# A second expert layer: 256 latent tokens dense in split products, or 160 dense in whole products and 96 gathered

## The chip, the core and the metric

One core of a Trainium2 chip runs the whole program. The metric is the device time of one execution in microseconds (us); the profile's times are counted from the first instruction of the span.

## The reference, cut to what matters

Two layers of a shared trunk run over 256 context tokens and 256 latent tokens of width 1024. Each layer ends in a retrieval of single-neuron experts out of 16384. Every token has 8 heads, each picks 16 experts, and what is added to the token is

```
u = jnp.take(expert_u, experts, axis=0)
v = jnp.take(expert_v, experts, axis=0)
act = jax.nn.gelu(jnp.einsum('td,ted->te', xb, u))
return jnp.einsum('te,ted->td', act * g, v)
```

where `g` is a softmax over the 16 scores of a head. In the second layer only the latent tokens go through this, and a last norm over them gives the output.

## The kernel before, in words

There are two ways to compute the experts, and both give the same sums. The dense way multiplies every expert with every token. A table A (tokens by experts, mostly zeros) holds the weights `g`, so that the output is (gelu(u x) * A) v. The gather way fetches the rows of a token's own experts: an indirect DMA on POOL's queue brings, for one of the 128 picks, one row of 4 KB for each of 128 tokens; VectorE multiplies and sums the row with the token (u), or adds it, scaled, to the token's sum (v).

In the first layer the context tokens go the gather way (`gather`, L1144) and the latents the dense way; the gather runs beside the latents' work. In the second layer all 256 latents go the dense way.

The dense way runs over 32 blocks of 512 experts. `hidden` (L978) makes one block of gelu(u x): four tiles of 512 KB of expert_ut, each with two of the eight slices of the contraction. The weights are TensorE's standing operand (128 experts), the 256 tokens stream. `value` (L1019) uses one block: four tiles of 512 KB of expert_v; here A's 128 tokens stand and 512 columns of v stream, for two token blocks and two halves of the width, into four accumulators in PSUM (`acc[b, h]`) that live through all 32 blocks. `scale` (L1011) multiplies a block of gelu with its part of A.

In the first layer the operands are whole fp32 (`whole=True`, `len(hT) == 1`). In the second, every operand is split into a high and a low fp32r part (`cut`, L210: ScalarE copies the high part at L215, VectorE subtracts at L148), and `mm3` (L320) issues three products for each, at L328, L329 and L330; `value` does so for A too (L1032, L1033) and issues its products at L1051.

`build` (L936) makes A from the picks, in chunks of 2, 3 and 3 parts of 16; for eight tokens at a time VectorE makes marks (L951 to L956), TensorE sums them with 16 small products (L964) and ScalarE writes them out (L966).

`peer_out` (L1054) writes the order. It first finishes the hidden blocks up to block 11, woven with the first chunk of A; then comes a loop over i = 0 to 31: `scale(i)`, `hidden(i + 8)` as long as there is one (from block 12 on, so in 20 of the 32 turns), and `value(i)`. After every tile's DMA a `step()` draws on the tasks beside: the builds of the other two chunks, and in the first layer the gather, each at a fixed rate for each step. Before `peer_out`, the heads' queries and picks (`peer_heads`) are woven with the first hidden blocks (`hiddens`), six in the second layer.

All dense tiles are loaded on SP's queue, in order. `dtile` (L193) takes four places of the pool "w" in turn; with whole operands every third tile comes from the pool "dw" instead. Each engine works through its own instructions in order. The gather has six places ("gx") and works four issues behind its newest (`lead`).

Of the kernel before, what the change touches and what calls it, by code (L numbers as in the profile page):

```python
# [36 lines left out]
NEG = -3.0e38  # L37

# [31 lines left out]
class Net:  # L70
# [690 lines left out]
    def peer_in(self, l, s, whole=False):  # L761
# [6 lines left out]
        st["hT"], st["done"] = hT, 0  # L768
        return st
# [166 lines left out]
    def build(self, st, s0, ns):  # L936

        j0, n = s0 * SUB, ns * SUB
        for i in range(ns):
            st["A", s0 + i] = self.va.tile([128, SUB, L], F32, name="A", bufs=4)  # L940
# [18 lines left out]
        def sums(ts, oi, oa):  # L959
            ps = self.psum()  # L960
            pv = ps[:, :TG * n].rearrange("p (t j) -> p t j", j=n)
            for u in range(TG):
                for i in range(2):
                    nc.tensor.matmul(pv[:, u, :], oi[:, u // TU, :, u % TU], oa[:, i, u // TU, :, u % TU], start=(i == 0), stop=(i == 1))  # L964
            for i in range(ns):
                nc.scalar.activation(st["A", s0 + i][:, :, ts].rearrange("p j t -> p t j"), pv[:, :, i * SUB:(i + 1) * SUB], AF.Copy, scale=1.0 / GS)  # L966
# [11 lines left out]
    def hidden(self, l, st, q):  # L978

        nc, hT = self.nc, st["hT"]  # L980
        ps = [self.psum() for i in range(2)]
        for k2 in range(4):
            w = self.dtile([128, 2, 512], len(hT) == 1)
            nc.sync.dma_start(w, self.t["expert_ut"][l, q, :, 2 * k2:2 * k2 + 2, :])
            u = (w,) if len(hT) == 1 else self.cut(w, [128, 2, 512])
            yield
            for kk in range(2):
                k = 2 * k2 + kk
                for j in range(4):

                    self.mm3(ps[j // 2][:, (j % 2) * L:(j % 2 + 1) * L], [x[:, kk, j * 128:(j + 1) * 128] for x in u], at_(hT, k),
                             k == 0 and j % 2 == 0, k == KD - 1)
        for i in range(2):
            if q < st.get("early", 0):
                if ("early", q // 4) not in st:
                    st["early", q // 4] = self.va.tile([128, SUB, L], F32, name="A", bufs=4)
                o = 4 * (q % 4) + 2 * i
                a = st["early", q // 4][:, o:o + 2, :]
            else:
                a = self.va.tile([128, 2, L], F32, name="act", bufs=2 * self.n["ahead"])  # L1000
            nc.scalar.activation(a, ps[i].rearrange("p (j t) -> p j t", j=2), AF.Gelu_apprx_tanh)  # L1001
            st["act", 2 * q + i] = a
# [16 lines left out]
    def value(self, l, acc, st, q, step):  # L1019

        nc, p = self.nc, self.vp
        A, o = st["A", 4 * q // SUB], 4 * q % SUB
        vt = self.t["expert_v"][l].rearrange("(j i) d -> i j d", i=NK)
        for j2 in range(2):
# [11 lines left out]
            for jj in range(2):  # L1036
# [9 lines left out]
                for x, b in todo:  # L1046
                    j = 4 * q + 2 * j2 + x
                    ts = slice(b * 128, (b + 1) * 128)
                    for n, (aa, ww) in enumerate(prods):
                        for h in range(2):  # L1050
                            nc.tensor.matmul(acc[b, h], aa[:, x, ts], v[x][ww][:, h * 512:(h + 1) * 512],  # L1051
                                             start=(j == 0 and n == 0), stop=(j == NK - 1 and n == len(prods) - 1))

    def peer_out(self, l, sets, late=None, beside=None, out=None):  # L1054
# [51 lines left out]
        for i in range(end):  # L1106
# [18 lines left out]
            elif i == end - 4 and l == DEPTH - 1:  # L1125

                self.gf, ga = [[self.va.tile([128, 512], F32, name="act", bufs=2 * ahead) for h in range(2)] for x in range(2)]
# [4 lines left out]
            if q == nq - 1:  # L1132
                for b in range(2):
                    for h in range(2):
                        nc.vector.tensor_tensor(out=acc[b, h], in0=acc[b, h], in1=ga[h], op=OP.mult)
                        xx = self.x[s, b][:, h * 512:(h + 1) * 512]
                        nc.vector.tensor_tensor(out=xx, in0=xx, in1=acc[b, h], op=OP.add)
                        self.square(s, b, h, xx, acc[b, h])
# [5 lines left out]
    def gather(self, l, s, st):  # L1144
# [9 lines left out]
        for row, col in zip(rows, (g, sh)):  # L1154
            self.row_of([row[:, 0:512], row[:, 512:D]], col)
        def room(name):
            return [self.pe.tile([128, D], F32, name=name, tag="hp", bufs=self.n["hp"]) for b in range(2)]
        hN, sums = room("hn"), None
        for b in range(2):
# [6 lines left out]
        jobs = [(w, b, r) for w in "uv" for r in range(nr) for b in range(2)]  # L1166
        tabs = {w: self.t["expert_" + w].rearrange("l e d -> (l e) d") for w in "uv"}
        got = []
        for i in range(len(jobs) + lead):
            if i < len(jobs):  # L1170
                w, b, r = jobs[i]
                x = gp.tile([128, D], F32, name="gx", bufs=n)
                nc.gpsimd.indirect_dma_start(x, None, tabs[w], bass.IndirectOffsetOnAxis(ap=idx[:, b, r:r + 1], axis=0),  # L1173
                                             element_offset=l * NK * NK * D)
                got.append(x)
            if i >= lead:
                w, b, r = jobs[i - lead]
                x = got.pop(0)
                if w == "u":
                    keep(nc.vector.tensor_tensor_reduce(out=x, in0=x, in1=hN[b], scale=1.0, scalar=0.0, op0=OP.mult, op1=OP.add,  # L1180
                                                        accum_out=coef[:, b, r:r + 1]))
                    if (r, b) == (nr - 1, 1):
                        nc.scalar.activation(coef, coef, AF.Gelu_apprx_tanh)
                        nc.vector.tensor_tensor(out=coef, in0=coef, in1=st["g"].rearrange("p b h r -> p b (h r)"), op=OP.mult)
                elif r == 0:
                    sums = sums or room("vsum")
                    nc.vector.tensor_scalar(sums[b], x, coef[:, b, 0:1], None, op0=OP.mult)
                else:
                    keep(nc.vector.scalar_tensor_tensor(sums[b], x, coef[:, b, r:r + 1], sums[b], op0=OP.mult, op1=OP.add))  # L1189
# [3 lines left out]
        for b in range(2):  # L1193
            nc.vector.tensor_tensor(out=sums[b], in0=sums[b], in1=ga, op=OP.mult)
            nc.vector.tensor_tensor(out=self.x[s, b], in0=self.x[s, b], in1=sums[b], op=OP.add)
# [5 lines left out]
        self.root(s, 2)  # L1201
# [15 lines left out]
def program(tc, t, out, dbg=None):  # L1217
    with ExitStack() as ctx:
# [18 lines left out]
        with pool("kc0") as net.kc:  # L1237
# [5 lines left out]
            net.n = dict(s1=2, b4=15, t4=4, s2=3, qz=1, hp=8, gt="hp", late=1, whole=1, gx=6, lead=4)  # L1243
# [9 lines left out]
        net.n = dict(s1=1, b4=4, t4=0, s2=2, hp=8, ahead=4, pre=4, gx=6, lead=4, dw=2)  # L1253
# [11 lines left out]
        with pool("pe1", "right") as net.pe:  # L1265
# [6 lines left out]
            net.n = dict(s1=1, b4=5, t4=0, s2=2, hp=4, ahead=8, pre=8)  # L1272
            wp = pool("wp2")
            net.wp = wp.__enter__()
            with pool("h1") as net.mp:
                sl = net.peer_in(1, "l")
                for _ in sl["fill"]:
                    pass
                run(net.by_head(net.peer_heads(1, "l", sl)), (net.hiddens(1, sl, 6), 3))
            net.io = None  # L1280
            with pool("v1") as net.vp:
                net.peer_out(1, [("l", sl)], out=out)
            wp.__exit__(None, None, None)
# [70 lines left out]
```

## Time and profile before

| | |
|---|---|
| three runs, median (range) | 3004.85 us (2996.38 to 3007.26) |
| the profiled execution | 2997.31 us, span 2995.5 us |
| busy TensorE, VectorE, ScalarE, POOL | 93%, 73%, 33%, 20% of the span |
| second layer, queries and picks | 2118 to 2307 us |
| second layer, rest of the hidden blocks | 2307 to 2377 us |
| second layer, loop over the value blocks | 2377 to 2986 us |
| first layer's loop, gather beside it | 957 to 1808 us |

PE is TensorE, PEld its load of the standing operand, DVE VectorE, ACT ScalarE. A whole fp32 product appears as two records (so 16 products as 32); `hph` and `hpl` are the high and low part of the tokens, `whi` and `wlo` those of the weights. [...] MB are millions of bytes.

### The profile page before, as it was taken

The numbers are of one execution on the slowest core, as the hardware profiler recorded it, in microseconds if no ns is written. First come the engines' busy times: TensorE is split into PE (matmuls) and PEld (weight loads), VectorE is DVE, ScalarE is ACT, GpSimd is POOL, SyncE is SP. The second block draws the span as 40 slices with busy tenths as digits, with TensorE's granted clock in tenths as the row PEclk, the third lists the DMA queues.
The fourth block names the chain that finished last, engine by engine and source line by source line (L and its number), as shares of the span: only waits on it lengthen the run. The fifth ranks groups of instructions, "written<-read, shape, count | busy, mean of one in ns | idle before, by whom it ended". The sixth has DMA issues, their size and how long they took to land.

```text
span 2995.5 us, 45775 instructions
## 1 busy us (share of the span) xinstructions
PE 2781.6 (93%) x17380; PEld 2232.5 (75%) x17380; DVE 2181.6 (73%) x4525; ACT 976.9 (33%) x1798; POOL 598.7 (20%) x528
## 2 busy tenths in 40 slices
PE   7999999977995899998999988899987999999998
PEld 3779787756883466665766637889887989999987
DVE  3656676767999787667976675866799978548755
ACT  4454312301113021001200005555533555446544
POOL 0000000056312555445755450000000000000000
PEclk8999999988996999999999999999998999999999
DMA  7664665599862999999999994444443555665564
GB/s 266 193 202 146 205 193 162 174 367 380 313 230 93 385 337 385 409 409 361 368 407 409 409 380 137 129 121 144 149 144 114 154 170 170 190 189 163 176 197 147
DMA packets 295708, 724.64 MB, mean 242 GB/s; under 512 B 26817, under 2 KB 147905, under 8 KB 295489
## 3 DMA queue, kind: packets, MB, share of 16 engines
q1 hardware_dynamic: 221760, 453.25, 46.2%
q0 software_dynamic: 73728, 268.47, 23.3%
q8 instruction: 137, 2.24, 0.3%
q14 instruction: 83, 0.67, 0.1%
HBM read 720.58 MB, written 1.05 MB: 241 GB/s over the span
## 4 chain that ended last, share of the span: by engine, by line
PE 51%; DMA 19%; DVE 18%; issue 7%; POOL 3%; ACT 2%; SPq 0%; DVEq 0%; POOLq 0%; ACTq 0%
PE ps L1051 13%; DMA gx<-in_expert_v,idx 12%; PE ps L325 8%; PE ps L328 7%; PE ps L330 7%; PE ps L329 7%; POOL gx L1173 3%; DVE gx L1180 2%; DVE vsum L1189 2%; DMA gx<-in_expert_u,idx 2%; PE ps L964 2%; DVE eid L885 2%; DVE wlo L148 2%; PE ps L542 1%; PE ps L175 1%
## 5 line engine op out<-in xcount | busy, mean ns | idle before, releaser
L148 DVE TENSOR_TENSOR wlo<-w,whi 128x1024 fp32r<-128x1024 f32 (+1 forms) x404 | 488.1, 1209 | 258.0 <-ACT whi L215 257.2
L215 ACT ACTIVATE whi<-w 128x1024 fp32r<-128x1024 f32 (+1 forms) x404 | 421.8, 1046 | 474.3 <-PE ps L329 281.3
L1173 POOL DMA_INDIRECT gx<-in_expert_u,idx x256 | 303.6, 1186 | 914.7 <-DVE coef L1180 514.8
L325 PE MATMUL ps<-hph,w 128*128 128x256 f32 x1888 | 427.8, 384 | 7.7 <-DMA w<-in_w_query 7.7
L1189 DVE SCALAR_TENSOR_TENSOR vsum<-gx,coef,vsum 128x1024 f32<-128x1024 f32 x254 | 323.9, 1285 | 131.8 <-DMA gx<-in_expert_v,idx 131.5
L325 PEld LDWEIGHTS ps<-hph,w 128*128 128x128 f32 x1888 | 360.2, 192 | 68.9 <-issue 15.0
L1180 DVE CUSTOM_DVE_ANT_0 gx<-gx,hn 128x1024 f32<-128x1024 f32 x256 | 308.7, 1224 | 89.9 <-DMA gx<-in_expert_u,idx 89.1
L330 PE MATMUL ps<-hph,wlo 128*128 128x256 f32 x1152 | 329.2, 287 | 22.0 <-DVE wlo L148 21.9
L328 PE MATMUL ps<-hph,whi 128*128 128x256 f32 x1152 | 333.4, 290 | 2.7 <-ACT whi L215 2.5
L1173 POOL DMA_INDIRECT gx<-in_expert_v,idx x256 | 283.5, 1108 | 242.5 <-DVE vsum L1189 186.9
L329 PE MATMUL ps<-hpl,whi 128*128 128x256 f32 x1152 | 328.4, 285 | 0.0
L1051 PE MATMUL ps<-w,A 128*128 128x512 f32 x680 | 304.6, 597 | 12.5 <-DVE A L1017 11.7
L1051 PEld LDWEIGHTS ps<-w,A 128*128 128x128 f32 x680 | 128.4, 191 | 163.5 <-issue 148.4
L330 PEld LDWEIGHTS ps<-hph,wlo 128*128 128x128 f32 x1152 | 222.7, 194 | 24.1 <-DVE wlo L148 24.1
L966 ACT ACTIVATE A<-ps 128x128 f32<-128x128 f32 x512 | 143.5, 426 | 267.7 <-PE ps L964 264.7
L328 PEld LDWEIGHTS ps<-hph,whi 128*128 128x128 f32 x1152 | 223.3, 194 | 4.3 <-ACT whi L215 3.3
L329 PEld LDWEIGHTS ps<-hpl,whi 128*128 128x128 f32 x1152 | 223.1, 194 | 0.5
L1001 ACT ACTIVATE act<-ps 128x512 f32<-128x512 f32 x112 | 65.9, 593 | 429.2 <-PE ps L325 398.5
L1051 PE MATMUL ps<-dw,A 128*128 128x512 f32 x344 | 159.4, 607 | 2.3 <-issue 1.2
L1051 PE MATMUL ps<-whi,Ah 128*128 128x512 f32 x512 | 160.5, 394 | 0.0
L1051 PE MATMUL ps<-wlo,Ah 128*128 128x512 f32 x512 | 158.0, 390 | 0.0
L1051 PE MATMUL ps<-whi,Al 128*128 128x512 f32 x512 | 157.7, 389 | 0.0
(283 smaller groups left out, 4932.7 us busy)
## 6 DMA issues: line engine op xcount, KB each, us to landing
w<-in_expert_ut SPq DMA_DIRECT2D x214, 512.0 KB, 4.5
w<-in_expert_v SPq DMA_DIRECT2D x213, 512.0 KB, 4.3
w<-in_w_in SPq DMA_DIRECT2D x134, 512.0 KB, 3.9
w<-in_w_mod SPq DMA_DIRECT2D x96, 512.0 KB, 4.7
w<-in_w_query SPq DMA_DIRECT2D x48, 512.0 KB, 4.4
dw<-in_expert_v SPq DMA_DIRECT2D x43, 512.0 KB, 6.8
dw<-in_expert_ut SPq DMA_DIRECT2D x42, 512.0 KB, 6.7
w<-in_w_out SPq DMA_DIRECT2D x24, 512.0 KB, 3.6
```

What stands on the lines that cost most here:

```text
L148: self.nc.vector.tensor_tensor(out=lo, in0=full, in1=hi, op=OP.subtract)
L215: nc.scalar.activation(hi, w, AF.Copy)
L325: nc.tensor.matmul(ps, wpairs[0], xpair[0], start=first, stop=last, skip_group_check=True)
L328: nc.tensor.matmul(ps, wh, xh, start=first, stop=False, skip_group_check=True)
L329: nc.tensor.matmul(ps, wh, xl, start=False, stop=False, skip_group_check=True)
L330: nc.tensor.matmul(ps, wl, xh, start=False, stop=last, skip_group_check=True)
L966: nc.scalar.activation(st["A", s0 + i][:, :, ts].rearrange("p j t -> p t j"), pv[:, :, i * SUB:(i + 1) * SUB], AF.Copy, scale=1.0 / GS)
L1001: nc.scalar.activation(a, ps[i].rearrange("p (j t) -> p j t", j=2), AF.Gelu_apprx_tanh)
L1051: nc.tensor.matmul(acc[b, h], aa[:, x, ts], v[x][ww][:, h * 512:(h + 1) * 512], start=(j == 0 and n == 0), stop=(j == NK - 1 and n == len( ...
L1173: nc.gpsimd.indirect_dma_start(x, None, tabs[w], bass.IndirectOffsetOnAxis(ap=idx[:, b, r:r + 1], axis=0), element_offset=l * NK * NK * D)
L1180: keep(nc.vector.tensor_tensor_reduce(out=x, in0=x, in1=hN[b], scale=1.0, scalar=0.0, op0=OP.mult, op1=OP.add, accum_out=coef[:, b, r:r + 1]))
L1189: keep(nc.vector.scalar_tensor_tensor(sums[b], x, coef[:, b, r:r + 1], sums[b], op0=OP.mult, op1=OP.add))
```

## The change

In the second layer the latents of `PART`, 0 to 127 and 224 to 255, go the dense way (T = 160), with whole fp32 operands; tokens 128 to 223 go through `gather`, beside the loop. For the 160, `hidden_n` and `value_n` replace `hidden` and `value`. In `hidden_n` the tokens stand and 512 experts stream: one product for each of eight slices for the 128 tokens, and for the other 32 tokens one in a quarter of TensorE's columns, four slices into four quarters at once (`tile_position`), after the second and the fourth tile. ScalarE copies both banks; TensorE turns the first with transposes and folds the four quarters of the second with a matrix of four stacked identities (`fold32`); then comes the Gelu. In `value_n` the 32 tokens use a quarter for each of the four tiles, after all four have been used for the 128 tokens; after the loop `last` adds the four quarters into partitions 96 to 127. Eight instead of six hidden blocks are woven with the heads. The table A is built for 160 tokens. In the first layer the gather's rows of norms and sums get places of their own ("hn") and "dw" has four places instead of two. Of the diff what bears on the order and the work:

```diff
+PART = ((0, 128), (224, 256))
...
-        for t0 in range(0, L, TG):
-            ts = slice(t0, t0 + TG)
-            now = ts, *marks(ts)
+        for t0, t1 in enumerate(x for a, b in st["toks"] for x in range(a, b, TG)):
+            now = slice(t0 * TG, t0 * TG + TG), *marks(slice(t1, t1 + TG))
...
     def hidden(self, l, st, q):
+        if st["T"] < L:
+            yield from self.hidden_n(l, st, q)
+            return
...
+    def fold(self):
+        nc = self.nc
+        self.fold32 = self.pe.tile([128, 32], F32, name="fold", bufs=1)
+        nc.vector.tensor_reduce(self.fold32, self.ident.rearrange("p (g t) -> p t g", g=4), axis=AX.X, op=OP.add)
+        self.last = self.pe.tile([128, 128], F32, name="last", bufs=1)
+        nc.vector.memset(self.last, 0.0)
+        nc.vector.tensor_copy(self.last[:, 96:128], self.fold32)
+
+    def hidden_n(self, l, st, q):
+        nc, (hT,) = self.nc, st["hT"]
+        (a0, b0), (a1, b1) = st["toks"]
+        pu = [self.psum() for i in range(2)]
+        u = []
+        for k2 in range(4):
+            w = self.dtile([128, 2, 512], True)
+            nc.sync.dma_start(w, self.t["expert_ut"][l, q, :, 2 * k2:2 * k2 + 2, :])
+            yield
+            for kk in range(2):
+                k = 2 * k2 + kk
+                nc.tensor.matmul(pu[0], hT[k // 4][:, k % 4, a0:b0], w[:, kk, :], start=(k == 0), stop=(k == KD - 1))
+                u.append((k, w[:, kk, :]))
+            if k2 % 2:
+                for k, x in u:
+                    g = 32 * (k % 4)
+                    nc.tensor.matmul(pu[1][g:g + 32, :], hT[k // 4][:, k % 4, a1:b1], x, start=(k < 4), stop=(k >= 4), tile_position=(0, g))
+                u = []
+        c = [self.va.tile([128, 512], F32, name="turn", bufs=4) for i in range(2)]
+        for i in range(2):
+            nc.scalar.activation(c[i], pu[i], AF.Copy)
+        for i in range(2):
+            pt = self.psum()
+            pv = pt[:, :2 * st["T"]].rearrange("p (j t) -> p j t", j=2)
+            for jj in range(2):
+                es = slice((2 * i + jj) * 128, (2 * i + jj + 1) * 128)
+                nc.tensor.transpose(pv[:, jj, 0:128], c[0][:, es], self.ident)
+                nc.tensor.matmul(pv[:, jj, 128:], c[1][:, es], self.fold32, start=True, stop=True)
+            self.gelu(st, q, i, pv)
...
+    def value_n(self, l, acc, st, q, step):
...
+        v = []
+        for jj in range(4):
+            j = 4 * q + jj
+            w = self.dtile([128, D], True)
+            nc.sync.dma_start(w, vt[:, j, :])
+            step()
+            for h in range(2):
+                nc.tensor.matmul(acc[0, h], A[:, o + jj, 0:128], w[:, h * 512:(h + 1) * 512], start=(j == 0), stop=(j == NK - 1))
+            v.append(w)
+        for h in range(2):
+            for jj in range(4):
+                g = 32 * jj
+                nc.tensor.matmul(acc[1, h][g:g + 32, :], A[:, o + jj, 128:160], v[jj][:, h * 512:(h + 1) * 512], start=(q == 0), stop=(q == NK // 4 - 1),
+                                 tile_position=(0, g))
...
+                        y, r = acc[b, h], slice(0, 128)
+                        if b and st["T"] < L:
+                            c = self.va.tile([128, 512], F32, name="turn", bufs=4)
+                            nc.scalar.activation(c, y, AF.Copy)
+                            y, r = self.psum(), slice(96, 128)
+                            nc.tensor.matmul(y, self.last, c, start=True, stop=True)
...
-                nc.gpsimd.indirect_dma_start(x, None, tabs[w], bass.IndirectOffsetOnAxis(ap=idx[:, b, r:r + 1], axis=0),
+                m = rows_of[b]
+                nc.gpsimd.indirect_dma_start(x[:m], None, tabs[w], bass.IndirectOffsetOnAxis(ap=idx[:m, b, r:r + 1], axis=0),
...
-            net.n = dict(s1=2, b4=15, t4=4, s2=3, qz=1, hp=8, gt="hp", late=1, whole=1, gx=6, lead=4)
+            net.n = dict(s1=2, b4=15, t4=4, s2=3, qz=1, hp=4, gt="hp", late=1, whole=1, gx=6, lead=4, hn=2)
...
-        net.n = dict(s1=1, b4=4, t4=0, s2=2, hp=8, ahead=4, pre=4, gx=6, lead=4, dw=2)
+        net.n = dict(s1=1, b4=4, t4=0, s2=2, hp=4, ahead=4, pre=4, gx=6, lead=4, hn=2, dw=4)
...
-            net.n = dict(s1=1, b4=5, t4=0, s2=2, hp=4, ahead=8, pre=8)
...
-                run(net.by_head(net.peer_heads(1, "l", sl)), (net.hiddens(1, sl, 6), 3))
...
-                net.peer_out(1, [("l", sl)], out=out)
...
+            net.n = dict(s1=1, b4=5, t4=0, s2=2, hp=4, ahead=8, pre=8, gx=6, lead=4, hn=2, dw=4)
+            with pool("g1") as net.gp:
+                net.fold()
+                with pool("h1") as net.mp:
+                    sl = net.peer_in(1, "l", whole=True, toks=PART)
...
+                    run(net.by_head(net.peer_heads(1, "l", sl)), (net.hiddens(1, sl, 8), 3))
+                net.io = None
+                with pool("v1") as net.vp:
+                    net.peer_out(1, [("l", sl)], beside=(net.gather(1, "l", sl, blocks=((1, 96),)), 264 / 200), out=out)
```

## Rows read from the trace of the kernel before

**Rows 1.** Stretches: us; busy PE, PEld, DVE, ACT, POOL; clock; DMA; GB/s.
```profile
957.00:1808.00 851.00, 813.43 (x3600) 517.37 (x3600) 635.50 (x880) 88.81 (x262) 454.90 (x399) 0.98 0.98 380
900.00:957.00 57.00, 26.80 (x523) 20.10 (x521) 55.97 (x178) 24.23 (x72) 3.60 (x3) 0.53 0.17 53
2118.00:2307.00 189.00, 160.77 (x1232) 157.51 (x1232) 172.97 (x592) 76.96 (x95) 0.00 (x0) 0.91 0.46 142
2307.00:2377.00 70.00, 64.47 (x903) 62.48 (x903) 67.03 (x171) 39.41 (x92) 0.00 (x0) 0.93 0.46 137
2377.00:2986.00 609.00, 608.93 (x4489) 541.87 (x4488) 421.46 (x590) 323.80 (x508) 0.00 (x0) 1.00 0.59 177
```

**Rows 2.** Timeline of TensorE, second layer's loop: start, length, engine, line, operation.
```profile
2614.59 0.28 PE L328 MATMUL ps<-hph,whi 128*128 128x256 f32 x1
...
2625.99 0.62 PE L1051 MATMUL ps<-whi,Ah 128*128 128x512 f32 x2
...
2636.90 0.28 PE L328 MATMUL ps<-hph,whi 128*128 128x256 f32 x1
```

**Rows 3.** Timeline of TensorE, first layer's loop.
```profile
1555.78 3.60 PE L1051 MATMUL ps<-dw,A 128*128 128x512 f32 x8
...
1569.51 0.81 PE L325 MATMUL ps<-hph,w 128*128 128x256 f32 x3
```

**Rows 4.** Timeline of TensorE, one set of the modulation's products in four quarters.
```profile
57.76 1.06 PE L175 MATMUL ps<-w,sc 128*32 128x512 f32 x8
58.75 0.69 PE L493 MATMUL ps<-zT,wa 32*128 32x256 f32 x2
```

**Rows 5.** Timeline of TensorE: four transposes and what follows; the scores of a head.
```profile
2000.21 0.60 PE L676 MATMUL ps<-fc,P 128*128 128x128 f32 x4
2000.56 0.36 PE L328 MATMUL ps<-hh,whi 128*128 128x256 f32 x1
...
2144.55 1.05 PE L834 MATMUL ps<-sk,qT 128*128 128x128 f32 x8
```

**Rows 6.** Building A: a timeline line of TensorE; two VectorE groups.
```profile
2324.42 0.97 PE L964 MATMUL ps<-oa,oi 128*128 128x32 f16 x32
...
L951 DVE TENSOR_TENSOR oi<-io,iT 128x1024 f16<-128x1024 f16 x63 | 43.5, 691 | 18.7 <-PE ps L964 18.3
L956 DVE TENSOR_TENSOR oa<-oj,ap 128x384 f16<-128x384 f16 x128 | 39.9, 354 | 0.0
```

**Rows 7.** Groups of the page: gather and Gelu; busy us, mean ns, idle before.
```profile
L1173 POOL DMA_INDIRECT gx<-in_expert_u,idx x256 | 303.6, 1186 | 914.7 <-DVE coef L1180 514.8
...
L1189 DVE SCALAR_TENSOR_TENSOR vsum<-gx,coef,vsum 128x1024 f32<-128x1024 f32 x254 | 323.9, 1285 | 131.8 <-DMA gx<-in_expert_v,idx 131.5
...
L1001 ACT ACTIVATE act<-ps 128x512 f32<-128x512 f32 x112 | 65.9, 593 | 429.2 <-PE ps L325 398.5
```

**Rows 8.** DMA from 1200 to 1360; last column: us from issue to landing.
```profile
DMA packets 17944, 65.42 MB, mean 409 GB/s; under 512 B 1992, under 2 KB 1992, under 8 KB 17937
...
gx<-in_expert_u,idx POOLq DMA_INDIRECT x32, 10.5
```

**Rows 9.** DMA from 600 to 740, gather's and SP's queue: packets, MB, share.
```profile
q0 software_dynamic: 9599, 34.97, 65.4%
q1 hardware_dynamic: 12373, 16.95, 34.6%
```

**Rows 10.** DMA from 2520 to 2690, the dense tiles of the second layer.
```profile
w<-in_expert_v SPq DMA_DIRECT2D x32, 512.0 KB, 4.3
```

**Rows 11.** TensorE's waits from 957 to 1808: us in total, times, longest.
```profile
PE ps L964 <- DVE oa L956: 23.3, 3, 11.2
PE ps L1051 <- DVE A L1017: 12.8, 2, 11.7
...
PE ps L1051 <- DMA w<-in_expert_v: 0.7, 1, 0.7
```

**Rows 12.** VectorE's groups from 2118 to 2307: its splits.
```profile
L148 DVE TENSOR_TENSOR wlo<-w,whi 128x1024 fp32r<-128x1024 f32 x48 | 58.5, 1218 | 11.7 <-ACT whi L215 11.7
```

More of the change, by code (lines that the diff above doesn't have):

```diff
@@ L768, in peer_in @@
         st["hT"], st["done"] = hT, 0
+        st["toks"], st["T"] = toks, sum(b - a for a, b in toks)
         return st
@@ L939, in build @@
         for i in range(ns):
[L940 removed]
+            st["A", s0 + i] = self.va.tile([128, SUB, st["T"]], F32, name="A", bufs=4)
         nc, p, io, iT, jT, ap = self.nc, self.vp, self.io, st["iT"], st["jT"], st["ap"]
@@ L993, in hidden @@
         for i in range(2):
[L994 to L1001, printed above, removed]
@@ L1002, in hidden, with gelu @@
-            st["act", 2 * q + i] = a
+            self.gelu(st, q, i, ps[i].rearrange("p (j t) -> p j t", j=2))
+    def gelu(self, st, q, i, src):
+        if q < st.get("early", 0):
+            if ("early", q // 4) not in st:
+                st["early", q // 4] = self.va.tile([128, SUB, st["T"]], F32, name="A", bufs=4)
+            o = 4 * (q % 4) + 2 * i
+            a = st["early", q // 4][:, o:o + 2, :]
+        else:
+            a = self.va.tile([128, 2, st["T"]], F32, name="act", bufs=2 * self.n["ahead"])
+        self.nc.scalar.activation(a, src, AF.Gelu_apprx_tanh)
+        st["act", 2 * q + i] = a
@@ L1019, in value @@
     def value(self, l, acc, st, q, step):
+        if st["T"] < L:
+            return self.value_n(l, acc, st, q, step)
         nc, p = self.nc, self.vp
@@ L1125, in peer_out @@
             elif i == end - 4 and l == DEPTH - 1:
-                self.gf, ga = [[self.va.tile([128, 512], F32, name="act", bufs=2 * ahead) for h in range(2)] for x in range(2)]
+                self.gf, ga = [[self.va.tile([128, 512], F32, name="fin", bufs=4) for h in range(2)] for x in range(2)]
                 for h in range(2):
@@ L1142, in peer_out, with gather @@
                         self.final(out, b)
-    def gather(self, l, s, st):
+    def gather(self, l, s, st, blocks=((0, 128), (1, 128))):
         nc, gp, keep = self.nc, self.gp, self.tc.keep_in_program_order
@@ L1155, in gather @@
             self.row_of([row[:, 0:512], row[:, 512:D]], col)
+        rows_of = dict(blocks)
         def room(name):
-            return [self.pe.tile([128, D], F32, name=name, tag="hp", bufs=self.n["hp"]) for b in range(2)]
+            return {b: gp.tile([128, D], F32, name=name, tag="hn", bufs=self.n["hn"]) for b in rows_of}
         hN, sums = room("hn"), None
-        for b in range(2):
+        for b in rows_of:
             nc.vector.scalar_tensor_tensor(hN[b], self.x[s, b], self.rs[s][:, b:b + 1], rows[0], op0=OP.mult, op1=OP.mult)
@@ L1165, in gather @@
         nr = 128
-        jobs = [(w, b, r) for w in "uv" for r in range(nr) for b in range(2)]
+        jobs = [(w, b, r) for w in "uv" for r in range(nr) for b in rows_of]
         tabs = {w: self.t["expert_" + w].rearrange("l e d -> (l e) d") for w in "uv"}
@@ L1192, in gather @@
         self.row_of([ga[:, 0:512], ga[:, 512:D]], self.modT[l][:, 40:48, si])
-        for b in range(2):
-            nc.vector.tensor_tensor(out=sums[b], in0=sums[b], in1=ga, op=OP.mult)
-            nc.vector.tensor_tensor(out=self.x[s, b], in0=self.x[s, b], in1=sums[b], op=OP.add)
+        for b, m in blocks:
+            xx, y = self.x[s, b][:m], sums[b][:m]
+            nc.vector.tensor_tensor(out=y, in0=y, in1=ga[:m], op=OP.mult)
+            nc.vector.tensor_tensor(out=xx, in0=xx, in1=y, op=OP.add)
+            if m < 128:
+                continue
             for h in range(2):
@@ L1200, in gather @@
             yield
-        self.root(s, 2)
+        if blocks[0][1] == 128:
+            self.root(s, 2)
         yield
```

44 lines of the change are left out of this document (21 added, 23 removed).

## The prediction

> **What bounds the kernel now.** I read the table of stretches first, because the change lies in the second layer's expert stage and an average over 3 ms says little about it [rows 1]. That stage has three parts: the queries with six hidden blocks (2118 to 2307), the rest of the hidden blocks with the first third of the coefficient table (2307 to 2377), and the loop over 32 value blocks (2377 to 2986). In the loop TensorE is busy for all of its 609 us at full clock, VectorE for 421 and the DMA for 59%: TensorE is the bound and nothing makes it wait. In the query part VectorE is busy 173 of 189 us. The reader then looks at the first layer's loop (957 to 1808), the nearest relative of what is planned: fp32 products with a gather beside them. There the DMA is full (0.98, 380 GB/s) and TensorE still has 813 busy us of 851.
>
> **Prices.** In the second layer a hidden block H takes 2625.99 - 2614.59 = 11.4 us and a value block V 10.9, a round 22.3 [rows 2]. In the first layer, with whole fp32 operands, V has 16 products of 128x512 and takes 1569.51 - 1555.78 = 13.7 us, so one product costs 0.86 [rows 3]. The quarter products have a relative too: the modulation's four 128*32 groups, eight records, 58.75 - 57.76 = 0.99 us until the next instruction [rows 4], against 3.44 for four full products. So quarters do run together. Four full transposes take 2000.56 - 2000.21 = 0.35 us; eight records of small fp32 products 1.05 [rows 5]. 32 products of the table build, two groups of tokens, take 0.97 [rows 6].
>
> **The new TensorE work.** New H: 8 full products at 0.86 = 6.9; two sets of four quarters at 0.99 and 0.1 for the change over, 2.2; then four transposes and four folding products, 0.35 + 0.8. These wait for ScalarE's copies of the two banks. The first copy runs under the last quarters; the second (0.59, as the 128x512 ScalarE row [rows 7]) cannot, so TensorE stands about 0.9 with the signals: bounds 0.6 and 2, the latter if ScalarE is at other work. Behind the waiting fold stand H's other folds and all of V; ScalarE's Gelu waits for the folds, but is needed only eight rounds later. H is 11.1. New V: 8 x 0.86 + 2.0 = 8.9. A round is 20.0 where it was 22.3; without late data 20 rounds and 12 V alone are 507 instead of 577 us. Builds: 40 groups instead of 64 in the loop, 20 us instead of 32.
>
> **What the loop gains in DMA.** A round loads 8 tiles of 0.524 MB, 4.2 MB. The gather has 256 issues of 96 rows of 4 KB, 0.393 MB each, at 264/200 a step, eight steps a round: 4.1 MB. The first layer's steady stretch moved 65.42 MB in 160 us, 409 GB/s [rows 8]. At that rate 8.3 MB need 20.4 us: as much as TensorE. [...]
>
> **Lateness.** Six tiles can be ahead: a w tile takes the place of the one six before it (every third has its own pool). V now holds its four tiles until its quarters end, so at the end of V only the next two are loaded. When both queues are backed up they serve about the same number of packets (9599 and 12373, where the dense ones were smaller) [rows 9]; with packets of 4 KB each side gets half, 204 GB/s, and a tile takes 2.6 us. Unloaded, a tile lands after 4.3 [rows 10], 1.3 of it transfer; so 3.0 + 2.6 = 5.6 us after the place is free. The two loaded tiles of H give 4.5 us of work: the third is 1.1 late, the fourth 0.9, V's last 0.3. SP's queue is in order, so a tile that waits for its place also holds the next one, even one with a free place. Where the third falls into the other pool it is early. I take 1.8 a round, from the bounds 0.4 (DMA alone) and 5 (both queues' tiles landing like the first layer's gathers, 10.5 us [rows 8], against 5.6). A round is 21.8. V alone, beside the gather: 2.5 late, 11.4; after the gather 9.6.
>
> **VectorE in the loop.** 256 gather operations at 1.29 at most [rows 7] are 330 us; 40 build groups at 0.69 + 3 x 0.355 [rows 6] are 70; the scaling some 30: 430 with the rest, where the splits (206 at 1.22) go. It isn't the bound, except while a build runs: 1.18 groups and 1.32 gathers a step are 3.8 us against TensorE's 3.1, over 18 steps: 12 us, twice. In the first layer such places cost TensorE 23.3 + 12.8 us [rows 11]. I take 24 together (bounds 5 and 36). Once, ScalarE's Gelu of the gather's coefficients waits for VectorE with the copies behind it; that lies in the same lag. POOL issues only gathers, 256 where there were none, 1.32 x 1.2 us [rows 7] of a step's 2.7, and nothing waits behind them.
>
> **The loop's sum.** 20 x 21.8 + 8 x 11.4 + 4 x 9.6 + 20 + 24 = 610 against 609: what TensorE saves, the data takes back.
>
> **Before and after the loop.** Query part: VectorE loses its 48 splits (1.22 each [rows 12]), 173 - 59 = 114 us; TensorE then has 8 queries (16 products of 256 columns at half of 0.86, 6.9, and the scores' 1.1) and eight H at 11.1, 153. With 11 for the first query and the last head that is 164 instead of 189: -25 (bounds -40 and -5), and two hidden blocks more are done. Rest: four H and 21 groups at 0.5 are 55, with 7 for the first marks 62; before, VectorE was busy for 67 of 70 [rows 1]: -8. After the loop block 1 goes through two more copies and two products of 0.86: +3. The fold's constants and the gather's norm rows (some 2.5 us of VectorE) lie beside the queries and the first V. In the first layer, the gather's own pool and two more dw buffers change no wait that its rows show (its TensorE waited 0.7 us for tiles [rows 11]); nothing, within 5.
>
> Sum: -25 - 8 + 1 + 3 = -29 on the profiled execution's 2997.3, which is 7.5 under the runs' median of 3004.85; so about 2975 on the median.
>
> **Rivals.**
> 1. The data are never late: the gather is paced by the program and leaves room, a round is DMA's 20.4 or less, V alone 9.5. The loop is 565, the result 2930. For it: in the first layer TensorE waited for almost no tile at 409 GB/s. Against it: there a tile held 3.4 us of work and was freed at once.
> 2. The tiles starve (slower). Place: the third and fourth tile of every H and V. If the gather takes more than its half, a tile takes 3.1 us instead of 2.6 and the round's eight 24.5; from a round of 23.3 on the change gives no gain, from 24.0 on it loses 0.5%. At 24.5 the loop is some 665 and the result 3030; at 25.5, 3050. For it: the gather always has five issues in flight, and a gather's landing of 10.5 us shows a long line.
> 3. The clock. TensorE's short pauses, repeated every round, could lower the granted clock, as between 900 and 957, where it was busy 27 of 57 us and the clock was 0.53 [rows 1]. If a fifth of the loop's 527 us of work ran at half clock, that adds 105 less what the data would have cost anyway (36 + 24), some 45: 3020; a tenth gives 3000. [...] Against it: in the first layer's loop, with 37 us of waits, 0.98 [rows 1, 11].
> 4. The change does not do what it says: the quarters of 32 columns run one after the other. 104 sets in the loop and 16 before it cost 2.4 us more each: 3260. The modulation's rows speak against it.
>
> **How the numbers follow.** About 0.5% (15 us) can be told from no change. Forecast 0.50, its own range 2945 to 3005: faster 0.36, same 0.14. Rival 1 0.22, all faster. Rival 2 0.17: slower 0.14, same 0.03. Rival 3 0.08: same 0.05, slower 0.03. Rival 4 0.03, slower. Faster 0.58, same 0.22, slower 0.20. The range reaches below to rival 1 with the lower bounds of the query part (-15) and of the builds (-19), 2895, and above to rival 2 with a round of 25.3, 3045. Outside stay rounds beyond that, the worst of rival 3, and 4.
>
> **What would show it.** Right: quarter products in sets of eight records of about 1 us; a TensorE gap of about 1 us ahead of each fold, released by ScalarE; H and V of 11 and 9 us in the loop with gaps before each third tile released by a DMA of an expert tile; a loop of about 610; a query part of 164; the DMA near 400 GB/s from 2340 on. Wrong: gaps of over 4 us a round at a DMA that isn't full (the holding, not the rate), TensorE waiting mostly for VectorE (the gather's lag), a loop under 570, or a clock under 0.9 in it.

## The result, and the profile after

| | median (range), runs |
|---|---|
| before, beside it on the same chip | 3000.61 us (2995.62 to 3007.26), 4 |
| after | 3114.21 us (3098.11 to 3123.82), 4 |
| ratio | 1.0384, interval 1.036 to 1.0408 |

The change costs 3.8%, where 1% less was forecast, and lies beyond the range. The profiled execution took 3123.82 us, its span is 3122.1.

The stretches of the changed kernel come first; the lines answer to [rows 1] (same columns). Its loop over the value blocks begins at 2336 and ends at 3109.

```profile
957.00:1808.00 851.00, 814.19 (x3638) 518.36 (x3634) 639.27 (x897) 91.44 (x270) 458.72 (x399) 0.98 0.97 379
2118.00:2276.00 158.00, 153.44 (x680) 96.60 (x681) 123.88 (x546) 33.08 (x57) 5.45 (x6) 0.96 0.63 197
2276.00:2336.00 60.00, 57.30 (x528) 29.95 (x529) 37.86 (x118) 22.30 (x64) 0.00 (x0) 0.94 0.44 150
2336.00:3109.00 773.00, 590.19 (x2561) 230.76 (x2559) 398.94 (x591) 78.61 (x211) 251.72 (x250) 0.89 0.98 265
```

The first layer is as before. The part ahead of the loop is 41 us shorter (158 + 60 instead of 189 + 70). The loop takes 773 us where 610 were forecast. In it the DMA share is 0.98, and yet only 265 GB/s are moved: in the first line the same share moves 379.

What TensorE waited for in that loop (us in total, times, longest); the first layer's loop is in [rows 11]:

```profile
PE ps L1035 <- DMA w<-in_expert_ut: 112.4, 39, 7.0
PE ps L1118 <- DMA w<-in_expert_v: 62.8, 17, 9.0
PE ps L967 <- DVE oa L959: 5.5, 5, 4.0
```

TensorE stands 181 us, 175 of them for dense tiles; with its 590 busy us that is nearly the whole loop. One round of its timeline (start, length, engine, line, operation, and in brackets the idle time before it) shows the work beside the waits:

```profile
2603.78 3.78 PE L1035 MATMUL ps<-w,hph 128*128 128x512 f32 x4 [5.66 <-DMA w<-in_expert_ut]
...
2615.19 1.98 PE L1035 MATMUL ps<-w,hph 128*128 128x512 f32 x4 [1.78 <-DMA w<-in_expert_ut]
2617.10 1.07 PE L1040 MATMUL ps<-w,hph 128*32 128x512 f32 x8
2618.10 0.44 PE L1050 MATMUL ps<-fc,turn 128*128 128x128 f32 x2
2618.37 1.02 PE L1118 MATMUL ps<-dw,A 128*128 128x512 f32 x2
2619.23 0.30 PE L1051 MATMUL ps<-fold,turn 128*128 128x32 f32 x2
...
2633.77 5.76 PE L1035 MATMUL ps<-w,hph 128*128 128x512 f32 x8 [5.49 <-DMA w<-in_expert_ut]
```

From the start of one hidden block to the next are 2633.77 - 2603.78 = 30.0 us, where 21.8 were forecast; over the loop's 20 hidden blocks (2397.6 to 2966.9) the mean is 30.0 too. The long wait stands ahead of a hidden block's first tile (5.66 and 5.49 us here; in all 53 of the 112 us of L1035), a shorter one ahead of a later tile. TensorE's prices are as forecast: a set of quarters takes 2618.10 - 2617.10 = 1.0, and the wait for ScalarE's copies ahead of the folds is filled by V's first products (L1118 between L1050 and L1051).

Last, the DMA's view of 2500 to 2900, to be read against [rows 8] (the queues with packets, MB, share of 16 engines; q0 is the gather's, q1 the dense tiles'):

```profile
DMA packets 30645, 109.77 MB, mean 274 GB/s; under 512 B 3890, under 2 KB 3890, under 8 KB 30626
...
q0 software_dynamic: 15444, 54.24, 51.3%
q1 hardware_dynamic: 15182, 55.28, 51.2%
```

The engines are full; it is the packet that is longer. 16 engines x 400 us x 1.025 / 30626 packets are 214 ns for one. In the first layer [rows 8] the two queues' shares are 64.1% and 38.4%, the same 1.025 together, and 16 x 160 x 1.025 / 17937 are 146. (Without the packets under 512 B it is 245 against 165; the expectations below count so.) That both queues carry the same number of packets is the program's own pace: 1.32 gathers of 0.393 MB for each dense tile of 0.524.

### The profile page after: what moved, and what is told of

It reads as the page before. It is cut to its first block, busy times and chain, and to the rows that moved or that the text cites. A ratio compares the mean times of both kernels' runs of the same rounds, so it can differ in the third digit from the quotient of the medians.

```text
span 3122.1 us, 39732 instructions
## 1 busy us (share of the span) xinstructions
PE 2746.9 (88%) x14528; PEld 1827.9 (59%) x14528; DVE 2082.2 (67%) x4435; ACT 672.2 (22%) x1436; POOL 853.9 (27%) x784
## 3 DMA queue, kind: packets, MB, share of 16 engines
HBM read 821.24 MB, written 1.05 MB: 263 GB/s over the span
## 4 chain that ended last, share of the span: by engine, by line
PE 36%; DMA 28%; DVE 16%; issue 12%; POOL 6%; ACT 2%; SPq 0%; another core or an unknown queue 0%; POOLq 0%; DVEq 0%; ACTq 0%
DMA gx<-in_expert_v,idx 15%; PE ps L327 8%; POOL gx L1256 6%; PE ps L330 4%; PE ps L331 4%; PE ps L332 3%; PE ps L1118 3%; DMA w<-in_expert_v 3%; DMA gx<-in_expert_u,idx 3%; DVE gx L1264 2%; PE ps L1035 2%; DMA w<-in_expert_ut 2%; DVE vsum L1274 2%; DVE eid L888 1%; PE ps L1103 1%
## 5 line engine op out<-in xcount | busy, mean ns | idle before, releaser
L1274 DVE SCALAR_TENSOR_TENSOR vsum<-gx,coef,vsum 128x1024 f32<-128x1024 f32 (+1 forms) x381 | 486.3, 1282 | 287.3 <-DMA gx<-in_expert_v,idx 282.3
L1264 DVE CUSTOM_DVE_ANT_0 gx<-gx,hn 128x1024 f32<-128x1024 f32 (+1 forms) x384 | 464.8, 1223 | 241.7 <-DMA gx<-in_expert_u,idx 231.5
L1103 PE MATMUL ps<-w,A 128*128 128x512 f32 x680 | 304.6, 597 | 12.4 <-DVE A L1067 11.8
L1035 PE MATMUL ps<-w,hph 128*128 128x512 f32 x340 | 200.3, 719 | 113.4 <-DMA w<-in_expert_ut 112.4
L1118 PE MATMUL ps<-w,A 128*128 128x512 f32 x344 | 180.8, 654 | 63.5 <-DMA w<-in_expert_v 62.8
L150 DVE TENSOR_TENSOR wlo<-w,whi 128x1024 fp32r<-128x1024 f32 (+1 forms) x132 | 155.4, 1179 | 113.0 <-ACT whi L217 112.4
L1035 PEld LDWEIGHTS ps<-w,hph 128*128 128x128 f32 x340 | 67.1, 219 | 204.8 <-DMA w<-in_expert_ut 147.6
L217 ACT ACTIVATE whi<-w 128x1024 fp32r<-128x1024 f32 (+1 forms) x132 | 134.7, 1024 | 167.5 <-PE ps L331 75.1
L330 PE MATMUL ps<-hh,whi 128*128 128x256 f32 (+1 forms) x520 | 152.7, 294 | 7.5 <-ACT whi L217 5.6
L327 PE MATMUL ps<-hph,dw 128*128 128x256 f32 x672 | 152.8, 380 | 0.0
L1118 PEld LDWEIGHTS ps<-w,A 128*128 128x128 f32 x344 | 65.2, 205 | 145.6 <-issue 91.7
L331 PE MATMUL ps<-hl,whi 128*128 128x256 f32 (+1 forms) x520 | 148.7, 286 | 0.7 <-DVE hl L150 0.7
L332 PE MATMUL ps<-hh,wlo 128*128 128x256 f32 (+1 forms) x520 | 148.8, 286 | 0.6 <-DVE wlo L150 0.6
```

Of the source, the lines that this page charges most:

```text
L150: self.nc.vector.tensor_tensor(out=lo, in0=full, in1=hi, op=OP.subtract)
L217: nc.scalar.activation(hi, w, AF.Copy)
L327: nc.tensor.matmul(ps, wpairs[0], xpair[0], start=first, stop=last, skip_group_check=True)
L330: nc.tensor.matmul(ps, wh, xh, start=first, stop=False, skip_group_check=True)
L331: nc.tensor.matmul(ps, wh, xl, start=False, stop=False, skip_group_check=True)
L332: nc.tensor.matmul(ps, wl, xh, start=False, stop=last, skip_group_check=True)
```

## The experiments

**Theory.** A gather of 96 rows is slow, for itself and for the dense tiles beside it, although it moves fewer bytes than one of 128. **Rivals:** the holding of four tiles for the quarters; two full queues, whatever their rows; the rising bytes. Where a run leaves out work, its result is another, and only its time is of use.

**Fetch 128 rows, use 96.**

```diff
-                m = rows_of[b]
+                m = max(rows_of[b], 128)
```

> Every gather of the second layer fetches 128 rows instead of 96; VectorE still uses 96 of them, the result is the same. Theory R (the number of rows in a gather sets how long every 4 KB packet takes, also the dense ones): packets go back from 240 to about 163 ns and the DMA from 274 to about 400 GB/s; a round moves 4.2 + 5.5 = 9.7 MB in 24 us, the loop is about 620 us instead of 773 and the kernel about 2970, though a third more rows are fetched. Theory S (two queues that are both backed up share the DMA badly, whatever the rows): 274 GB/s stays, a round is 35 us, the kernel 3200 or more. Theory H (the tiles are held too long and the DMA merely follows): rounds stay at 30 us, 3110.

Measured: 2988.09 us, ratio 0.9949 (0.9932 to 0.9967) to the kernel before, with a third more gathered bytes than the change. Its loop, TensorE's waits there, and the DMA from 2500 to 2800:

```profile
2330.00:2973.00 643.00, 550.97 (x2565) 220.87 (x2563) 397.60 (x591) 79.18 (x211) 298.12 (x250) 0.95 0.95 370
```

```profile
PE ps L1035 <- DMA w<-in_expert_ut: 39.2, 27, 3.7
PE ps L1118 <- DMA w<-in_expert_v: 25.5, 11, 4.4
PE ps L1050 <- ACT turn L1044: 18.0, 1, 18.0
```

```profile
DMA packets 31427, 114.60 MB, mean 382 GB/s; under 512 B 3490, under 2 KB 3490, under 8 KB 31410
...
q0 software_dynamic: 17981, 65.47, 55.8%
q1 hardware_dynamic: 13429, 48.90, 42.1%
```

A gather packet now costs 16 x 300 x 0.558 / 17981 = 149 ns, a dense one 150, where the change had 213 and 216. In full slices of that window the profile gives 409 GB/s. One number took 130 us from the loop (773 to 643). That is theory R, though the kernel is 18 us over its 2970 and the loop 23 over its 620. The 18.0 us are the one wait foreseen as "Once, ScalarE's Gelu of the gather's coefficients waits for VectorE with the copies behind it" (ScalarE waited 38.2 us for them): here it stands by itself. The queues carry 65.47 and 48.90 MB, 1.34 to 1, again the program's pace and not one half each.

**No gather at all** (tokens 128 to 223 get no experts added).

```diff
-                    net.peer_out(1, [("l", sl)], beside=(net.gather(1, "l", sl, blocks=((1, 96),)), 264 / 200), out=out)
+                    net.peer_out(1, [("l", sl)], out=out)
```

> Leaves out the second layer's gather, so tokens 128 to 223 get no experts there. Theories R and S: without the gather a round is 20.0 to 20.5 us and V alone 9 to 9.6, the loop 530 to 560, the kernel about 2890. Theory H: TensorE still waits for tiles by several us a round, rounds over 24 us and a loop over 620.

Measured: 2859.26 us, ratio 0.9526 (0.9501 to 0.9552). The loop, and TensorE's only wait in it:

```profile
2324.00:2841.00 517.00, 515.95 (x2562) 213.05 (x2561) 81.86 (x202) 77.12 (x208) 0.00 (x0) 1.00 0.59 206
```

```profile
PE ps L1118 <- DMA w<-in_expert_v: 0.4, 2, 0.2
```

517 us at clock 1.00, a little under the 530 to 560 expected, and most rounds at 19.4: holding four tiles for the quarters costs nothing where the DMA has room (a share of 0.59), and TensorE's terms (20 x 20.0 + 12 x 8.9 + 20 = 527) were right. It also prices the change's clock: the same products took 590 us at 0.89, 74 more.

**The kernel before, with 96 of 128 rows in the first layer's gather** (64 context tokens get no experts).

```diff
-                nc.gpsimd.indirect_dma_start(x, None, tabs[w], bass.IndirectOffsetOnAxis(ap=idx[:, b, r:r + 1], axis=0),
+                x = x[:96]
+                nc.gpsimd.indirect_dma_start(x, None, tabs[w], bass.IndirectOffsetOnAxis(ap=idx[:96, b, r:r + 1], axis=0),
...
```

> The kernel before, where the first layer's gather fetches and uses 96 of the 128 rows of each block (it leaves out 64 of the 256 context tokens). A quarter fewer bytes. Theory R: packets of the first layer's loop go from 163 to about 240 ns, 409 to about 272 GB/s, and that loop, with some 271 MB, takes about 990 us instead of 850: the kernel some 130 us longer, 3130. Theories S and H, which lie in the second layer's new code: not longer than before, 2960 to 3000.

Measured: 3210.18 us, ratio 1.0695 (1.0659 to 1.0732): a quarter of the gathered bytes less, and 7% slower. The DMA from 1200 to 1360, the window of [rows 8]:

```profile
DMA packets 12383, 44.37 MB, mean 277 GB/s; under 512 B 1571, under 2 KB 1571, under 8 KB 12375
...
q0 software_dynamic: 6311, 22.17, 51.7%
q1 hardware_dynamic: 6064, 22.09, 51.5%
```

With none of the change in it the rate falls from 409 to 277. Quarters, tiles of the second layer and its order have no part in that. The kernel lost more than the 130 us expected: its loop takes 1031 us (998 to 2029) where [rows 1] have 851, and begins 41 us later. TensorE hardly waited for tiles there (1.1 us), but for VectorE (86.9 us for the marks of A, 69.5 for A's scaling).

**64 rows**, fetched and used (`blocks=((1, 64),)`; tokens 192 to 223 get no experts).

> The gather of the second layer fetches and uses 64 rows (it leaves out tokens 192 to 223): 6.95 MB a round. If the packet time grows as the rows get fewer (R, by the count): 240 ns or more, 270 GB/s or less, a round of 25.5 us or more. If only row counts that 8 times a whole number of engines can't carry are slow, or if the slow packets need both queues full (S): about 163 ns, a round near TensorE's 20.5 us and the kernel near 2900.

Measured: 3060.62 us, ratio 1.0197 (1.0172 to 1.0222), 251 GB/s from 2500 to 2800, on theory R's side. With half the rows of a full gather the kernel is still slower than with 128 fetched (2988.09).

**112 rows** fetched, 96 used (`max(rows_of[b], 112)`).

> The second layer's gather fetches 112 rows of which 96 are used; the result is the same. If the packet time falls evenly from 96 rows to 128, about 200 ns: 330 GB/s for 9.0 MB a round, 27 us, the kernel about 3055. If only 128 is good: 220 to 245 ns, 285 GB/s, a round of 31 us, the kernel 3140.

Measured: 3154.3 us, ratio 1.0519 (1.0464 to 1.0574): slower than 96, at 278 GB/s, and near the 3140 of "only 128 is good". The loss doesn't shrink step by step as the rows come nearer to 128.

**Transfers alone.** Four small kernels, each run once, issue 32 transfers to a stretch, with six places for each kind. The two calls in the first of them (g and d are the rows):

```python
nc.gpsimd.indirect_dma_start(x[:g], None, tab, bass.IndirectOffsetOnAxis(ap=idx[:g, i:i + 1], axis=0))
...
nc.sync.dma_start(w[:d], vt[:d, (n * N + i) % 256, :])
```

> Computes nothing of the reference: nine stretches of 32 gathers and/or 32 plain tile loads of 4 KB rows, six places each, a barrier between: gather of 128 rows alone; 96 alone; tile of 128 alone; then a tile of 128 rows with gathers of 128, 96, 112 and 64; then a tile of 96 with a gather of 96; a tile of 96 alone. Theory R1 (a transfer of 96 rows is slow by itself): packets of 240 ns in the second and the last stretch too. Theory R2 (slow only where two streams of differently divided rows run side by side): about 163 ns in all that run alone, in 128 with 128 and in 96 with 96; 240 ns in 96 with 128, and slow in 112 and 64 with 128.

The totals of six stretches; in order: gather of 128, gather of 96, tile of 128, both of 128, 96 beside a tile of 128, tile of 96:

```profile
DMA packets 4605, 16.78 MB, mean 384 GB/s; under 512 B 510, under 2 KB 510, under 8 KB 4604
DMA packets 3579, 12.58 MB, mean 251 GB/s; under 512 B 507, under 2 KB 507, under 8 KB 3579
DMA packets 4606, 16.78 MB, mean 396 GB/s; under 512 B 510, under 2 KB 510, under 8 KB 4605
DMA packets 9213, 33.56 MB, mean 400 GB/s; under 512 B 1023, under 2 KB 1023, under 8 KB 9211
DMA packets 8193, 29.38 MB, mean 282 GB/s; under 512 B 1023, under 2 KB 1023, under 8 KB 8191
...
DMA packets 3585, 12.61 MB, mean 251 GB/s; under 512 B 510, under 2 KB 510, under 8 KB 3582
```

96 rows alone (251 GB/s) take longer than 128 (12.58 MB / 251 = 50 us against 44), on either queue, and beside a full tile the sum falls from 400 to 282. Two queues aren't needed for that: it is theory R1. Over the four kernels stretches of 128 rows alone moved 383 to 396 GB/s, those of 96 alone 244 to 275.

> A kernel of DMA stretches alone, 32 transfers of rows of 4 KB in each, one after the other: gathers of 128, 120, 112, 96 (partitions 0 to 95), 96 (partitions 32 to 127), 80, 64 and 32 rows; plain tiles of 120, 112 and 64 rows; at last a gather of 120 beside a tile of 128. It computes nothing of the reference. Theory (a transfer of fewer than 128 rows is slow by itself, whatever the number): 128 at 380 to 400 GB/s and about 166 ns a packet; 120, 112, 96, 80, 64 all at 245 to 290 GB/s and 230 to 275 ns, so that 120 rows take longer than 128; where the partitions begin makes no difference (96 at 32 to 127 as 96 at 0 to 95, within 5%); plain tiles as gathers. Rival (the bytes fall unevenly on the 16 DMA engines, some of which have no work while others have one row more): the GB/s follow the rows in steps, 120 and 112 at 350 or more, 64 at 200 or less, and 112 never longer than 128.

Gathers of 120, 96, 80 and 64 rows, all at partition 0:

```profile
DMA packets 4603, 15.72 MB, mean 250 GB/s; under 512 B 766, under 2 KB 766, under 8 KB 4603
...
DMA packets 3579, 12.57 MB, mean 261 GB/s; under 512 B 511, under 2 KB 511, under 8 KB 3579
...
DMA packets 3067, 10.48 MB, mean 247 GB/s; under 512 B 508, under 2 KB 508, under 8 KB 3067
...
DMA packets 2553, 8.40 MB, mean 205 GB/s; under 512 B 504, under 2 KB 504, under 8 KB 2552
```

120 rows take 63 us, longer than 128; 80 and 64 (42 and 41 us) hardly less than 128. The rival's steps are out (120 at 250, not 350). The theory misses in three places: 64 moves 205, half the full rate, where 245 to 290 were expected; 112 moves 224 as a gather and 279 as a plain tile, so the two aren't alike there; and 96 at 32 to 127 moves 244, 7% less than at 0 to 95.

> Again a kernel of DMA stretches alone, 32 steps in each, which computes nothing of the reference. Plain tiles: 96 rows of 4 KB; 128 rows of 3 KB (the same bytes); 128 of 2 KB; 64 of 4 KB; 64 of 8 KB; 96 of 8 KB; then 128 rows of 4 KB as a transfer of 96 and one of 32; 128 of 4 KB in one; at last gathers: 128 rows in one, and as 96 and 32. Theory (what counts is that a transfer fills all 128 partitions, not its bytes): 128 rows of 3 KB at 370 GB/s or more, a quarter faster than the 96 of 4 KB with the same bytes at 250; 64 and 96 of 8 KB at 300 or less; the split 96 and 32 no better than 300, since each part is a short transfer. Rival 1 (a fixed cost for each transfer, so that smaller ones are slower): 128 of 3 KB at 300 or less, 64 of 8 KB and 96 of 8 KB at 370 or more. Rival 2 (what counts is which partitions lie in flight together): the split 96 and 32 at 370 or more, which would be a cure without extra bytes.

Tiles: 96 rows of 4 KB, 128 of 3 KB, 64 of 8 KB, and 128 rows as 96 and 32:

```profile
DMA packets 3579, 12.58 MB, mean 258 GB/s; under 512 B 509, under 2 KB 509, under 8 KB 3578
DMA packets 4609, 12.59 MB, mean 377 GB/s; under 512 B 512, under 2 KB 512, under 8 KB 4608
...
DMA packets 2561, 16.80 MB, mean 204 GB/s; under 512 B 511, under 2 KB 511, under 8 KB 511
...
DMA packets 5116, 16.78 MB, mean 237 GB/s; under 512 B 1023, under 2 KB 1023, under 8 KB 5114
```

The same 12.58 MB go at 377 GB/s in 128 rows and at 258 in 96. Rows of 8 KB don't help (204 with 64, 263 with 96), so it is no fixed cost of a transfer; nor does it help to send the missing 32 rows separately. Not all 128-row stretches are fast: with rows of 2 KB it was 291 GB/s, at a queue share of 0.88. The split gather moved 209, but its queue was busy for 72% only, so it tells nothing.

> DMA stretches alone once more, 32 transfers of rows of 4 KB in each; nothing of the reference is computed. Plain tiles into partitions 0 to 63, 32 to 95, 64 to 127, 0 to 31, 16 to 111, 0 to 95, 0 to 127; gathers into 0 to 63 and 32 to 95; then a gather into 32 to 95 and one into 0 to 63, each beside a tile of 128 rows. So far 64 rows at 0 to 63 moved 204 GB/s, half of what 128 rows move, and took 1.28 us each, as long as 128 rows. Theory (it counts in which partitions the rows land, since the halves 0 to 63 and 64 to 127 have ways of their own, and rows 0 to 31 share those of 32 to 63): 0 to 63 and 64 to 127 at 205 again, but 32 to 95, with half of its rows in each half, at 350 or more, as plain tile and as gather, and beside 128 rows above 370 in all where 0 to 63 beside 128 stays at 283. Rival (the number of rows alone counts): 205 for all three places of 64, and no difference beside the tile. [...]

Tiles of 64 rows into partitions 0 to 63, then 32 to 95; at last gathers of 64 rows beside a full tile, into 32 to 95, then into 0 to 63:

```profile
DMA packets 2551, 8.39 MB, mean 206 GB/s; under 512 B 505, under 2 KB 505, under 8 KB 2550
DMA packets 2559, 8.39 MB, mean 327 GB/s; under 512 B 511, under 2 KB 511, under 8 KB 2558
...
DMA packets 7140, 25.07 MB, mean 397 GB/s; under 512 B 1022, under 2 KB 1022, under 8 KB 7138
DMA packets 7166, 25.18 MB, mean 291 GB/s; under 512 B 1022, under 2 KB 1022, under 8 KB 7164
```

The number of rows alone isn't it: 64 rows go at 206 or 327 GB/s, and leave their neighbour at full speed (397) or not (291), by the partitions into which they fall. 64 to 127 is as slow as 0 to 63 (203), and 32 rows into 0 to 31 move 200, no less than the 64 of 0 to 63. The 327 falls short of the 350 expected. The gather into 32 to 95 alone is a miss too: 208 GB/s, but its queue filled only 69% of the engines, and POOL issued one every 1.19 us (0.89 of it busy) without a pause, so the issuing held it there. 96 rows into 16 to 111 gave 275, as into 0 to 95.

**The consequence: 128 dense and 128 gathered.** A full gather needs 128 tokens, so the 32 in quarters go the gather way too: `PART = ((0, 128),)`, no quarters and no folds, and the blocks of the gather ((1, 128)).

> 128 latents dense without quarters and folds, the other 128 gathered with 128 rows; the result is the same. Theory R (the DMA at about 409 GB/s is the bound): the loop moves 109 + 134 MB, 595 us at the least, some 610 with its start, against 643 of the run with 128 rows and 609 of the kernel before; the query part and the rest as there; the kernel 2945 to 2965. If TensorE's or VectorE's order were the bound instead: as the run with 128 rows, 2988.

Measured: 2944.81 us, ratio 0.9827 (0.9804 to 0.9849), at the lower edge of what theory R had. Its loop takes 589 us (2315 to 2904) at a DMA share of 1.00 and 390 GB/s, so the bytes bound it, while beside the queries the changed kernel's DMA moves only 197. The second version begins the gather there:

```diff
+rows = net.gather(1, "l", sl, blocks=((1, 128),))
-run(net.by_head(net.peer_heads(1, "l", sl)), (net.hiddens(1, sl, 8), 3))
+run(net.by_head(net.peer_heads(1, "l", sl)), (net.hiddens(1, sl, 8), 3), itertools.chain(iter(range(4)), itertools.islice(takes(rows, 3), 6)))
...
+net.peer_out(1, [("l", sl)], soon=(itertools.islice(rows, 16),), beside=(rows, 230 / 200), out=out)
```

> As the one before, but the gather begins beside the queries (some 17 issues) and the rest of the hidden blocks (16), where the DMA is at half, and runs in the loop at 230/200 a step. Theory R: 17 MB less in the loop, 226 MB, 553 us and some 15 for the start; the query part up to 10 us longer for VectorE; the kernel 2905 to 2930. If the bound is elsewhere, no faster than the one before.

Measured: 2920.54 us, ratio 0.9737 (0.972 to 0.9753), within the expected range. Its loop, first a full stretch of it, then all (568 us were expected):

```profile
2350.00:2600.00 250.00, 188.99 (x663) 78.70 (x664) 161.43 (x308) 25.87 (x79) 101.84 (x100) 0.95 1.02 407
2340.00:2912.00 572.00, 422.64 (x1440) 176.15 (x1440) 356.31 (x527) 57.20 (x169) 229.31 (x222) 0.95 1.00 395
```

> As the version with 128 tokens dense and 128 gathered, begun early, but five gathers for each head beside the queries and 32 in the rest of the hidden blocks, where that had three and 16. Some 25 issues of 0.524 MB less in the loop are 13 MB, at 407 GB/s 32 us less of DMA in it. Theory (the loop is bound by the bytes): a loop of 540 to 555 instead of 572, the query part and the rest 10 to 25 longer by VectorE's work of 1.29 us for each gather; together 2900 to 2925. Rival (VectorE bounds the part before the loop): 2925 to 2945.

Measured: 2917.3 us, ratio 0.9735 (0.9714 to 0.9755). Its loop (2357 to 2905) is still full, at 392 GB/s, and 24 us shorter than the 572 above, but begins 17 us later (2357 for 2340). Both lie within what was expected; the ratio is that of the version above, so most of what the loop gave, the part ahead of it took back. All three versions beat both kernels.

## Why the prediction was wrong, step by step

**The step that failed** is "The first layer's steady stretch moved 65.42 MB in 160 us, 409 GB/s [rows 8]. At that rate 8.3 MB need 20.4 us". The row is right, but the gathers and the dense tiles in it all filled 128 partitions; half of the new loop's bytes come in transfers of 96. Both together moved 274 GB/s: 8.3 MB / 274 = 30.3 us, the round of 30.0 that the timeline shows. The rate was carried over as if bytes alone set it. The whole miss lies in the loop: it is 163 us longer than forecast, the rest of the sum 8 us shorter, and 163 - 8 = 155 is what lies between the profiled execution (3123.82) and the forecast for one (2997.3 - 29 = 2968). That it is the rate, and the rate by the number of rows, is shown by the run with 128 rows fetched: 409 GB/s again in full slices of it, and 130 of the 163 us gone, with more bytes.

**Why 96 is slow**, as far as shown. What counts is into which partitions the rows fall, not only how many they are: 64 rows go at 206 GB/s into 0 to 63 and at 327 into 32 to 95. One transfer (a stretch divided by 32) takes 0.65 us with 32 rows in 0 to 31, 1.28 with 64 in 0 to 63, 1.29 with 64 in 64 to 127, 0.80 with 64 in 32 to 95, and 1.35 with 128. So in these runs the second 32 rows of 0 to 63 take as long again as the first (1.28 against 0.65), while the two halves together take hardly longer than one (1.35 against 1.28 and 1.29), and 64 rows with half in each lie nearer to 32 rows in one half than to 64 (0.80 against 0.65 and 1.28). What in the chip does this isn't shown. Two things stay open: by these times 64 rows in 32 to 95 should take 0.65 us and not 0.80, and 96 to 120 rows should take no longer than 128, where stretches of them took 46 to 67 us against 42 to 44.

**TensorE's work** was right: 517 us without the gather against 527, 1.0 for a quarter set. The 0.9 us for ScalarE's copies was mostly not there, since products of V came between. Two of its readings are loose, without weight: the folds' 0.8 is the distance to the next instruction (2144.55 to 2145.35) and not the 1.05 that the text gives, and by such distances 32 products of the build are 0.81 and not 0.97.

**The wait for tiles, lateness.** That with packets of 4 KB "each side gets half" isn't shown. The equal packets of the two queues (15444 and 15182) follow from the program's pace; with 128 rows they were 17981 and 13429, and in the window of [rows 8] 11226 and 6711. The holding of tiles and SP's order, 1.8 a round: not seen without the gather (0.4 us in all); with it they can't be told from the missing rate.

**Before the loop** 41 instead of 33 us less: right in kind. After it 3109 to 3122.1 is 13 us where it was 9.5: +3, as forecast. VectorE's lumps, 24: in the changed kernel such waits are 5.5 us, where the tiles come late anyway. With 128 rows fetched they are 7.4, and 25 with the 18.0 of the Gelu: near the size of the term, but most of it from the Gelu, which the prediction had put into the same lag.

**Rivals.** Rival 2 had TensorE starved for tiles, but neither the place nor the cause: the long waits stand ahead of the first tile of H about as much as ahead of the others, nothing shows that the gather takes more than its half, and the worst round of 25.5 fell short of 30.0. The clock of rival 3 did fall, to 0.89, in company with the 175 us of waits. The half clock that rival 3 reckons with is seen from 2603 to 2608, behind the wait of 5.66 us: 0.51, and four records in 3.78 us. Behind the wait of 1.78, from 2615 to 2618, it was 1.00, and four records took 1.98. The clock isn't the bound, because the DMA was full (0.98) and the round is DMA's 30.3. Without waits (no gather) it was 1.00. Rival 4 is out: a set took 1.0 us. (Twelve hidden blocks ahead of the loop have 24 sets, not 16, so its price would have been some 20 us higher.)

## What to carry to other kernels

Before a row's GB/s is carried over, compare the shape of its transfers with the new ones: the number of partitions that they fill, and which (64 rows went at 206 GB/s into 0 to 63, at 327 into 32 to 95), and not bytes alone. A gather of 64 to 120 rows from partition 0 on cost here nearly as much as one of 128, or more (41 to 66 us for 32 of them, against 43 to 44); fetch rows that nobody needs (130 us of the loop here), or choose the split so that it fills 128 (2944.81 us here, where the change takes 3114.21). When the DMA share stands near one at a lower GB/s, look at the time of a packet (214 ns here against 146), not for more overlap.

## What was not expected of the hardware

- 96 rows of 4 KB take longer than 128 (46 to 52 us against 42 to 44 for 32 transfers), 120 longer still (63 and 67), on both queues.
- A short transfer slows a full one beside it: 400 GB/s for 128 + 128, 282 for 96 + 128, 291 for 64 + 128 at partition 0, 397 for 64 + 128 at partition 32.
- 128 rows of 3 KB run at 377 GB/s where the same bytes in 96 rows of 4 KB run at 258.
